# Two transformer blocks with expert layers: the end of the second mixer in a fixed order, rows stored as normed, scale and shift behind the gather

## The chip, the cores and the metric

The kernel runs on one core of a Trainium2 chip as one program. The metric is the device time of one execution in microseconds. The kernel before takes 2361.54 us, the median of three runs (2360.82 to 2361.91).

## What is computed

512 tokens of 1024 features pass through two blocks. Each block is a mixer and an expert layer. The change works in the end of the second mixer, in the lists of both expert layers, and in how the second expert layer gets its tokens:

```python
y = merge_branches(o_a, o_b, g_a, g_b, w_out_a, w_out_b, w_o)   # ends in a projection by w_o
x = x + gt1 * rmsnorm(y, g_post_mix)
h2 = rmsnorm(x, g_pre_ffn) * (1 + sc2) + sh2
logits = h2 @ w_router + b_router
top_logits, top_e = lax.top_k(logits, 4)                        # of 32 experts
top_w = softmax(top_logits)
f = sum over experts of top_w * (gated unit of (h2 @ w_gu + b_gu)) @ w_dn + b_dn, for its tokens
x = x + gt2 * rmsnorm(f, g_post_ffn)
```

The first expert layer has 16 experts, two for a token; the second has 32 experts of 12 weight pieces of 1 MB each.

## The kernel before

The stages run one after the other: first mixer, first experts, second mixer, second experts. Matmuls with full accuracy are made from three products: a weight piece is split into a high part (`whi`, a ScalarE copy, L120) and the rest (`wlo`, a VectorE subtraction, L121), the left side likewise, and TensorE multiplies high by high, high by low and low by high (`mm3`, L85).

**End of the second mixer** (`mixer2`, from L2152). The projection by w_o is made in eight blocks: two column halves, in each four blocks of 128 tokens (`out_mm`, L2171), 24 matmuls for a block. Behind a block ScalarE sums the squares and VectorE multiplies by a row of gains (`rows[0]`, L2178, L2179). `tail_norm` (L2182) waits for both halves of a block. VectorE adds the two sums and computes an inverse root (`rsqrt`, L146: a chain of small operations on VectorE, each waiting for the last), adds the residual (L2187); GpSimd multiplies by a second row (L2188) and stores the residual; ScalarE sums the squares again (L2192), and a second root follows (L2193). `tail_turn` (L2195) transposes a block by TensorE, copies it by ScalarE (L2199) and makes the 32 router logits (`logits`, L770). `tail_u` (L2203) applies root, scale and shift on VectorE and stores the finished rows to U2 through GpSimd's DMA queue. Then come top-8 for each block (`top8`, L787), the routing weights, one-hot masks and their sums (`weights_of`, L799), and `lists` (L812): positions of the tokens in each expert by matmuls with a triangle, and, in `aux`, each token's number and its weight in three bf16 parts (`w3`, L918). This part is not in a manual order: a scheduler orders it, mixed with the next stage.

**Expert stages** (`experts`, L1302). The expert order and all steps are written out by hand, as a list of weight pieces `seq` and of hooks at steps; step 0 is the first piece, and steps below 0 run ahead of the first matmul. Weight pieces go into eleven buffers of 1 MB in the second stage. Four of the first ten loads are issued at step -11 on GpSimd's queue, the others on SP's (`AHEAD`, `BEHIND`). The first expert (two in the first stage) has a fixed place. For it `prep` (step -17) makes the one-hot tile (`list_hot`, L926) from the positions, `prep2` (-14) sums with `aux` by TensorE (`list_sum`, L933), `prep3` (-13) makes the row indices and weights (`list_end`, L940), and `x_gather` (-12, L994) gathers the rows by an indirect DMA from GpSimd. `prep` also has GpSimd make the tile `bsel` (L2267) that selects the expert's bias lane. `x_turn` (L999) transposes four of eight column groups into PSUM at steps -4 and -2, and `x_split` (L1010) half a step later copies them to the high part by ScalarE and subtracts by VectorE; blocks of 64 or 32 tokens (`col`) are only copied by ScalarE. The `plan` (L842), a generator, orders the other experts by their counts, on GpSimd with TensorE transposes and matmuls; its pieces run at the steps of `PLAN`, and the loads of the other experts wait for the number `exi` that it writes. The 32 places of the second stage take 128 tokens (four of them, two with a second block of 64), 96 (ten), 64 (ten) or 32 (eight).

## Time and profile before

| | us |
|---|---|
| median of three runs | 2361.54 |
| the profiled execution | 2365.56 |
| its span, first to last instruction | 2363.7 |
| TensorE, VectorE, ScalarE, GpSimd busy in it | 2118.9, 1385.6, 1024.0, 432.8 |
| HBM read and written in it | 642 MB and 35 MB |

Times below are microseconds from the span's start. The page cuts the span into 40 slices of 59.1 us; a digit is a busy share in tenths. In a timeline, a row has its start, its length, the engine, the line, the operation and `out<-in`, with sizes in partitions by elements; a bracket gives the idle time before it and what ended that. Rows of a window give the busy time of each engine with the count of instructions, the granted share of TensorE's full clock, the mean busy share of the 16 DMA engines and GB/s. Copies between engines appear under the helper's line, so `L83` is any matmul and the tile names tell which.

### The profile page before, as it was taken

How to read it: one execution, taken by the hardware profiler on the slowest of the kernel's cores; microseconds unless marked ns; L12 is line 12 of the kernel's file. 1: busy time of each engine (PE TensorE's matmuls, PEld its weight loads, DVE VectorE, ACT ScalarE, POOL GpSimd, SP SyncE). 2: the span in 40 equal slices, each digit the busy share in tenths (PEclk: the TensorE clock that was granted, in tenths of full speed). 3: DMA queues.
4: the chain of work that ended last, by engine and by line, in shares of the span. 5: the costliest groups of instructions: out<-in, count | busy, mean ns of one | idle time of the engine just before them, and what ended most of it. 6: DMA issues, size and time to landing. Idle time of an engine off the chain costs nothing. (4 is left out here: it accounts for less than half of the span.)

```text
span 2363.7 us, 31489 instructions
## 1 busy us (share of the span) xinstructions
PE 2118.9 (90%) x11221; PEld 1357.3 (57%) x11221; DVE 1385.6 (59%) x2687; ACT 1024.0 (43%) x1560; POOL 432.8 (18%) x405
## 2 busy tenths in 40 slices
PE   6999996779997999999987989979999997999993
PEld 2656664446665887778865445635555563554551
DVE  5555597645786856664466456545455553654663
ACT  3332454435674544553234444424344433443553
POOL 2001223311312120000024211312211031112100
PEclk9999896989998999999997999989999998999996
DMA  9766446998986423313357999999999989999996
GB/s 291 241 205 237 177 172 257 353 355 309 356 292 205 103 76 111 109 58 118 130 181 282 383 405 399 363 375 403 403 395 395 405 342 379 403 401 398 398 409 229
DMA packets 174659, 679.80 MB, mean 288 GB/s; under 512 B 21293, under 2 KB 61061, under 8 KB 116129
## 3 DMA queue, kind: packets, MB, share of 16 engines
q1 hardware_dynamic: 151632, 606.83, 67.5%
q0 software_dynamic: 22576, 69.85, 10.6%
q8 instruction: 90, 1.47, 0.3%
q10 hardware_dynamic: 288, 1.05, 0.1%
q14 instruction: 73, 0.59, 0.1%
HBM read 642.29 MB, written 35.46 MB: 287 GB/s over the span
## 5 line engine op out<-in xcount | busy, mean ns | idle before, releaser
L121 DVE TENSOR_TENSOR wlo<-wraw,whi 128x1024 fp32r<-128x1024 f32 (+1 forms) x535 | 646.3, 1232 | 333.7 <-ACT whi L120 324.6
L120 ACT ACTIVATE whi<-wraw 128x1024 fp32r<-128x1024 f32 (+1 forms) x535 | 552.6, 1055 | 344.5 <-PE pm L83 124.7
L83 PE MATMUL pm<-whi,xh 128*96 128x512 f32 (+1 forms) x704 | 283.9, 404 | 15.1 <-ACT whi L120 15.0
L83 PE MATMUL pm<-wlo,xh 128*96 128x512 f32 (+1 forms) x704 | 281.0, 402 | 6.1 <-DVE wlo L121 5.5
L83 PE MATMUL pm<-wraw,xh 128*32 128x512 f32 (+1 forms) x1344 | 238.3, 617 | 12.6 <-DMA wraw<-in_w_gu 12.6
L83 PE MATMUL pm<-whi,xl 128*96 128x512 f32 (+1 forms) x608 | 243.0, 400 | 0.0
L996 POOL DMA_INDIRECT xg<-U,ig x52 | 88.5, 1701 | 631.2 <-issue 275.8
L1240 POOL DMA_INDIRECT Y<-eo,isc x52 | 99.2, 1908 | 402.8 <-ACT eo L1239 103.2
L83 PEld LDWEIGHTS pm<-whi,xh 128*96 128x96 f32 (+1 forms) x704 | 125.3, 178 | 64.3 <-ACT whi L120 20.4
L83 PEld LDWEIGHTS pm<-wraw,xh 128*32 128x32 f32 (+1 forms) x1344 | 68.1, 126 | 151.3 <-issue 124.0
L83 PEld LDWEIGHTS pm<-wlo,xh 128*96 128x96 f32 (+1 forms) x704 | 119.6, 170 | 50.3 <-DVE wlo L121 8.8
L83 PE MATMUL po<-wlo,ah 128*96 128x512 f32 (+1 forms) x304 | 124.2, 409 | 12.7 <-DVE wlo L121 12.4
L83 PE MATMUL po<-wraw,ah 128*32 128x512 f32 (+1 forms) x672 | 132.6, 620 | 1.9 <-DMA wraw<-in_w_dn 1.9
L83 PE MATMUL po<-whi,ah 128*96 128x512 f32 (+1 forms) x304 | 126.8, 417 | 8.1 <-ACT whi L120 6.3
L83 PEld LDWEIGHTS pm<-whi,xl 128*96 128x96 f32 (+1 forms) x608 | 106.4, 175 | 36.8
L83 PE MATMUL po<-whi,al 128*96 128x512 f32 (+1 forms) x304 | 121.8, 401 | 0.8 <-DVE al L1204 0.8
L1008 PEld LDWEIGHTS pt<-ident,xg 64*128 64x128 f32 (+3 forms) x416 | 56.5, 199 | 100.8 <-issue 51.8
L1008 PE MATMUL pt<-ident,xg 64*128 64x64 f32 (+3 forms) x416 | 70.0, 294 | 47.8 <-DMA xg<-U,ig 47.1
L1017 ACT ACTIVATE xh<-pt 128x384 fp32r<-128x384 f32 (+2 forms) x56 | 28.2, 504 | 130.1 <-PE pt L1008 114.8
L83 PE MATMUL px<-hh,whi 128*128 128x512 f32 x192 | 77.3, 403 | 0.6 <-DVE gsum L766 0.6
L83 PE MATMUL px<-hh,wlo 128*128 128x512 f32 x192 | 76.6, 399 | 0.0
L83 PE MATMUL px<-hl,whi 128*128 128x512 f32 x192 | 76.6, 399 | 0.0
(630 smaller groups left out, 3774.1 us busy)
## 6 DMA issues: line engine op xcount, KB each, us to landing
wraw<-in_w_gu SPq DMA_DIRECT2D x254, 1024.0 KB
wraw<-in_w_dn SPq DMA_DIRECT2D x126, 1024.0 KB
wraw<-in_w_e_down SPq DMA_DIRECT2D x31, 1024.0 KB
wraw<-in_w_e_gate SPq DMA_DIRECT2D x30, 1024.0 KB
wraw<-in_w_e_up SPq DMA_DIRECT2D x30, 1024.0 KB
wraw<-in_w_in SPq DMA_DIRECT2D x58, 512.0 KB
mz<-in_w_ada SPq DMA_DIRECT2D x80, 256.0 KB
wraw<-in_w_mod SPq DMA_DIRECT2D x26, 512.0 KB
```

The source lines that it names most:

```text
L83: self.nc.tensor.matmul(out, lhsT, rhs, start=start, stop=stop)
L120: nc.scalar.activation(h, v, AF.Copy)
L121: nc.vector.tensor_sub(l, v, h.bitcast(F32))
L996: self.nc.gpsimd.indirect_dma_start(out=B.xg[0:B.n, :], out_offset=None, in_=self.U, in_offset=bass.IndirectOffsetOnAxis(ap=B.ig[:, :1], a ...
L1008: self.nc.tensor.transpose(B.xt[:, k * n:k * n + n], B.xg[0:n, 4 * h2 + k:1024:8], self.ident[0:n, 0:n])
L1017: nc.scalar.activation(B.xh[:, d, 0:n], pv, AF.Copy)
L1240: nc.gpsimd.indirect_dma_start(out=self.Y[:, :], out_offset=bass.IndirectOffsetOnAxis(ap=B.isc[:, :1], axis=0), in_=o, in_offset=None, com ...
```

## The change

The end of the second mixer is written in one order for TensorE, VectorE, ScalarE and GpSimd (`manual_schedule` orders the instructions of the region for each engine; where those of other regions fall among them is left to the scheduler). The norms, transposes and logits of a block stand between the matmuls of later blocks. Two roots are made together (`root`), and one multiplication of the root is folded into its constants. The rows are stored as normed, by ScalarE, without scale and shift; the last two stores leave on SP's queue. Scale and shift are applied to the gathered and transposed rows in `x_split`, four VectorE operations for each half of a block, each with one column of scale and shift; the copy of `col` blocks by ScalarE goes. In both stages the indices of the fixed experts are made ahead of the routing weights (`lists_first`, `lists_comb`), and of the fixed experts' hooks only `prep` and `x_gather` are left. The plan's first four pieces move to steps -11 to -8, and until `exi` is written they run on VectorE in the second stage. The lane selectors are made at the start of the kernel. `warm` adds twelve small matmuls whose result nobody reads. The diff, cut:

```diff
@@ -31,7 +31,7 @@
-PLAN = {2: (-4, -3, -1, 0, 1, 2), 1: (-4, -3, -1, 0, 1, 2)}
+PLAN = {2: (-11, -10, -9, -8, 1, 2), 1: (-4, -3, -1, 0, 1, 2)}
 
...
+    def rsqrt_steps(self, v, n, eps, scale=1.0, out=None):
+
+
+        ve = self.nc.vector
         a, t, y0, y1, y2, y3 = [self.tiny.tile([128, 8], F32, name=f"rs{i}")[:, :n] for i in range(6)]
-        ve.tensor_scalar(a, v, scale, eps, op0=OP.mult, op1=OP.add)
-        ve.tensor_scalar(y0.bitcast(I32), a.bitcast(I32), -0.5, 1597463007.0, op0=OP.mult, op1=OP.add)
-        for i, (y, z, k) in enumerate(((y0, y1, 3.0), (y1, y2, 12.0), (y2, y3, 768.0))):
+        y3 = y3 if out is None else out
+        ve.tensor_scalar(a, v, -scale, -eps, op0=OP.mult, op1=OP.add)
+        yield
+        ve.tensor_scalar(y0.bitcast(I32), a.bitcast(I32), -0.5, 519682224.0, op0=OP.mult, op1=OP.add)
+        yield
+        for i, (y, z) in enumerate(((y0, y1), (y1, y2), (y2, y3))):
             if n == 1:
                 ve.scalar_tensor_tensor(t, y, a, y, op0=OP.mult, op1=OP.mult)
             else:
                 ve.tensor_mul(t, y, y)
+                yield
                 ve.tensor_mul(t, t, a)
-            if i == 2:
-                ve.tensor_scalar(y, y, -1.0 / 8192, None, op0=OP.mult)
-            ve.scalar_tensor_tensor(z, t, k, y, op0=OP.subtract, op1=OP.mult)
+            yield
+            ve.scalar_tensor_tensor(z, t, 3 * 0.5 ** (2 * (13 / 27, 4 / 9, 1 / 3)[i]), y, op0=OP.add, op1=OP.mult)
+            yield
         return y3
+
+    def rsqrt(self, *a, **kw):
+        return self.run_mod(self.rsqrt_steps(*a, **kw))
+
+    def together(self, *gs):
+
+        gs, r = list(gs), [None] * len(gs)
+        left = list(range(len(gs)))
+        while left:
+            for i in list(left):
+                try:
+                    next(gs[i])
+                except StopIteration as e:
+                    r[i] = e.value
+                    left.remove(i)
+        return r
...
+
+        self.ehalf = cp.tile([128, 2], F32, name="ehalf")
+        for s in range(2):
+            nc.vector.memset(self.ehalf[64 - 64 * s:128 - 64 * s, s:s + 1], -1.0)
+            for a in (2 * s, 2 * s + 1):
+                ps = slice(32 * a, 32 * a + 32)
+                nc.vector.tensor_scalar(self.ehalf[ps, s:s + 1], self.pcol[ps, :], -32.0 * a, None, op0=OP.add)
...
+    def warm(self, n):
+
+        ps = self.pt.tile([128, 512], F32, name="pt")
+        for _ in range(n):
+            self.mm(ps[:, 0:128], self.ident, self.ident, True, True)
+
...
+    def mask_steps(self, E, K, xf, oh, c0, n):
+
+        nc, cs = self.nc, slice(c0, c0 + n)
+        nc.vector.tensor_tensor(oh[:, cs], self.slots[:, None, None, 0:E].to_broadcast([128, n, K, E]),
+                                xf[:, cs, 0:K, None].to_broadcast([128, n, K, E]), op=OP.is_equal)
+        yield
+        with nc.allow_low_precision(reason="sums of zeros and a one"):
+            nc.vector.reduce_sum(self.L.mask[:, cs, :], oh[:, cs].rearrange("p c k e -> p c e k"), axis=AX)
+        yield
+
...
+    def lists_first(self, n, tile):
+
+        L = self.L
+        L.first, ohs, ps = [], [], []
+        for b in range(n):
+            ohs.append(self.list_hot(L.pos[:, :, b:b + 1], 128, tile(b)))
+            ps.append(self.list_sum(ohs[b], lambda c: L.aux[:, c, b, 0:3], 3))
+        for b in range(n):
+            L.first.append(self.list_rows(ps[b], 128, self.lsm, b))
+        return ohs
+
+    def lists_comb(self, ohs):
+
+        nc, L = self.nc, self.L
+        aux = L.aux
+        self.w3(aux[:, :, :, 3], aux[:, :, :, 4], aux[:, :, :, 5], L.comb, [128, 4, L.E])
+        for b, oh in enumerate(ohs):
+            ps = self.list_sum(oh, lambda c: aux[:, c, b, 3:6], 3)
+            w = self.lsm.tile([128, 1], F32, name=f"slw{b}")
+            nc.vector.reduce_sum(w, ps[:, 0:3], axis=AX)
+            L.first[b].append(w)
 
     def plan(self, fixed, pairs):
 
 
         nc, sm, L = self.nc, self.esm, self.L
-        ve, E = nc.gpsimd, L.E
+        ve, E = (nc.vector if L.E == 32 else nc.gpsimd), L.E
...
         if B.col:
-            nc.scalar.activation(B.xf[:, d, 0:n], pv, AF.Copy)
+            lo = B.xf[:, d, 0:n]
+        else:
+            lo = B.xh[:, d, n:2 * n] if B.dual else B.xl[:, d, 0:n]
+        if self.xcols:
+
+            g, s = self.xcols
+            f = lo if B.col else pv
+            for k in range(4):
+                j = 4 * h2 + k
+                nc.vector.tensor_scalar(f[:, k, :], pv[:, k, :], g[:, j:j + 1], s[:, j:j + 1], op0=OP.mult, op1=OP.add)
+            pv = f
+        elif B.col:
+            nc.scalar.activation(lo, pv, AF.Copy)
+        if B.col:
             return
         nc.scalar.activation(B.xh[:, d, 0:n], pv, AF.Copy)
-        lo = B.xh[:, d, n:2 * n] if B.dual else B.xl[:, d, 0:n]
...
+            if b < fixed:
+                B.ig, B.isc, B.w = L.first[b]
+            else:
+                B.oh = self.list_hot(pos, B.n)
...
                 for i, f in enumerate(((prep, b, B), (prep2, B), (prep3, B), (self.x_gather, B))):
-                    at(max(s0 - lead[i] - o, p0 + i), *f)
+                    if b >= fixed or i in (0, 3):
+                        at(max(s0 - lead[i] - o, p0 + i), *f)
...
-        mask, comb = self.weights_of(16, 2, ex, w, self.lsm, sm.tile([128, 128], F32, name="ohk"))
-        self.lists(16, mask, comb)
+        oh = sm.tile([128, 4, 2, 16], F32, name="ohk")
+        self.lists(16)
+        self.run_mod(self.mask_steps(16, 2, ex, oh, 0, 4))
+        self.lists_pos()
+        ohs = self.lists_first(FIXED[1], tile)
+        self.comb_of(16, 2, w, oh)
+        self.lists_comb(ohs)
 
...
-            nc.gpsimd.dma_start(self.dap(RW, n * 1024, [[8, 128], [1, 8]]), a)
+            if n != 1:
+                nc.gpsimd.dma_start(self.dap(RW, n * 1024, [[8, 128], [1, 8]]), a)
             ca.append(a)
-        R = self.router([(t["w_router_2"][0], t["b_router_2"], 0, 32)], sm, ca[1], self.col(self.mod2, 3, "rwc"))
+        self.xcols = ca[1], self.col(self.mod2, 3, "rwc")
+        R = self.router([(t["w_router_2"][0], t["b_router_2"], 0, 32)], sm, *self.xcols)
...
-        rows = [rt[:, i, :] for i in range(3)]
-        self.bcast_row(rows[0], self.dap(RW, 0, [[1, 1024]]))
-        self.bcast_row(rows[1], self.dap(RW, 1024, [[1, 1024]]))
-        self.bcast_row(rows[2], self.dap(self.mod2, 3 * 1024, [[1, 1024]]))
+        row = rt[:, 0, :]
+        self.bcast_row(row, self.dap(RW, 0, [[1, 1024]]))
...
-        rr = sm.tile([128, 4], F32, name="rr")
+            nc.vector.tensor_mul(d, ps, row[:, hf * 512:hf * 512 + 512])
+
+
+        nv = sm.tile([128, 5, 2], F32, name="nv")
+        nr = sm.tile([128, 5, 2], F32, name="nr")
+
+        def root(c):
+            a, b = (1 if c == 4 else 0), (1 if c == 0 else 2)
+            return self.rsqrt_steps(nv[:, c, a:b], b - a, 1e-6, 1.0 / 1024, nr[:, c, a:b])
+
+        def tail_sum(c):
+            nc.vector.tensor_add(nv[:, c, 0:1], ss[:, 2 * c:2 * c + 1], ss[:, 2 * c + 1:2 * c + 2])
+
         def tail_norm(c):
             cs = slice(c * 128, c * 128 + 128)
             yc = y[:, c, :]
-            nc.vector.tensor_add(ss[:, 2 * c:2 * c + 1], ss[:, 2 * c:2 * c + 1], ss[:, 2 * c + 1:2 * c + 2])
-            r = self.rsqrt(ss[:, 2 * c:2 * c + 1], 1, 1e-6, 1.0 / 1024)
-            nc.vector.scalar_tensor_tensor(yc, yc, r, xr[c // 2][:, c % 2, :], op0=OP.mult, op1=OP.add)
-            nc.gpsimd.tensor_mul(xr[c // 2][:, c % 2, :], yc, rows[1])
+            nc.vector.scalar_tensor_tensor(yc, yc, nr[:, c, 0:1], xr[c // 2][:, c % 2, :], op0=OP.mult, op1=OP.add)
 
             nc.gpsimd.dma_start(self.out[0, cs, :] if c % 2 else self.X3[c * 64:c * 64 + 128, :], yc)
             q = w4t("q4", 1024)
-            nc.scalar.activation(q, yc, AF.Square, accum_out=ss[:, 2 * c + 1:2 * c + 2])
-            nc.vector.tensor_copy(rr[:, c:c + 1], self.rsqrt(ss[:, 2 * c + 1:2 * c + 2], 1, 1e-6, 1.0 / 1024))
+            nc.scalar.activation(q, yc, AF.Square, accum_out=nv[:, c + 1, 1:2])
+
+        uTs = {}
 
         def tail_turn(c):
             uT = rt[:, 3, :] if c % 2 else bg.tile([128, 1024], F32, name="uT", tag="L")
-            uT = uT.rearrange("p (k q) -> p k q", k=8)
+            uT = uTs[c] = uT.rearrange("p (k q) -> p k q", k=8)
...
-            self.logits(R, c, uT, rr[:, c:c + 1])
+
+        def tail_logits(c):
+            w = pw.tile([128, 1024], F32, name="pw")
+            return self.logits_mm(R, uTs[c], w[:, 0:512], w[:, 512:1024])
+
+        def logit_end(c, ps):
+            nc.vector.scalar_tensor_tensor(R.lg[:, c, :], ps, nr[:, c + 1, 1:2], R.br, op0=OP.mult, op1=OP.add)
 
         def tail_u(c):
+
             q = xr[c // 2][:, c % 2, :]
-            nc.vector.scalar_tensor_tensor(q, q, rr[:, c:c + 1], rows[2], op0=OP.mult, op1=OP.add)
-            nc.gpsimd.dma_start(self.U2[c * 128:c * 128 + 128, :], q)
-
+            nc.scalar.activation(q, y[:, c, :], AF.Copy, scale=nr[:, c + 1, 1:2])
+            (nc.sync if c > 1 else nc.gpsimd).dma_start(self.U2[c * 128:c * 128 + 128, :], q)
+
+        L = self.lists(32)
+        top = self.top_tiles(sm, "r")
+        w = sm.tile([128, 4, 4], F32, name="rw4")
+        s = sm.tile([128, 4, 1], F32, name="rs4")
         W = wo_half(0)
         for c in range(4):
-            out_mm(c, 0, W)
+            out_end(c, 0, out_mm(c, 0, W))
         W = wo_half(1)
-        for c in range(5):
-            if c < 4:
-                out_mm(c, 1, W)
-            if c:
-                tail_norm(c - 1)
-        for c in range(4):
-            tail_turn(c)
-            tail_u(c)
-
-        lg = R.lg
-        em, ex = self.top8(lg, sm, "r")
-        w = sm.tile([128, 4, 4], F32, name="rw4")
-        s = sm.tile([128, 4, 1], F32, name="rs4")
-        nc.vector.tensor_tensor(w, em[:, :, 0:4], em[:, :, 0:1].to_broadcast([128, 4, 4]), op=OP.subtract)
-        nc.scalar.activation(w, w, AF.Exp)
-        nc.vector.reduce_sum(s[:, :, 0], w, axis=AX)
-        nc.vector.reciprocal(s, s)
-        nc.vector.tensor_tensor(w, w, s.to_broadcast([128, 4, 4]), op=OP.mult)
-        mask, comb = self.weights_of(32, 4, ex, w, self.lsm, w4t("ohk", 512))
-        self.lists(32, mask, comb)
+        with self.tc.manual_schedule(engines={ET.PE, ET.DVE, ET.Activation, ET.Pool}):
+            for c in range(2):
+                out_end(c, 1, out_mm(c, 1, W))
+            tail_sum(0)
+            self.run_mod(root(0))
+            tail_norm(0)
+            out_end(2, 1, out_mm(2, 1, W))
+            tail_sum(1)
+            self.run_mod(root(1))
+            tail_norm(1)
+            tail_turn(0)
+            ps = out_mm(3, 1, W, None, range(4))
+            l0 = tail_logits(0)
+            tail_turn(1)
+            tail_sum(2)
+            self.run_mod(root(2))
+            tail_norm(2)
+            logit_end(0, l0)
+            tail_u(0)
+            out_end(3, 1, out_mm(3, 1, W, ps, range(4, 8)))
+            l1 = tail_logits(1)
+            tail_turn(2)
+            tail_sum(3)
+            self.run_mod(root(3))
+            l2 = tail_logits(2)
+            tail_u(1)
+            tail_norm(3)
+            logit_end(1, l1)
+            logit_end(2, l2)
+            self.top8(R.lg, sm, "r", 0, 3, top)
+            tail_turn(3)
+            ohk = w4t("ohk", 4, 4, 32)
+            self.together(root(4), self.mask_steps(32, 4, top[2], ohk, 0, 3))
+            l3 = tail_logits(3)
+            self.warm(8)
+            logit_end(3, l3)
+            self.top8(R.lg, sm, "r", 3, 1, top)
+            self.run_mod(self.mask_steps(32, 4, top[2], ohk, 3, 1))
+            tail_u(2)
+            tail_u(3)
+            nc.vector.tensor_tensor(w, top[0][:, :, 0:4], top[0][:, :, 0:1].to_broadcast([128, 4, 4]), op=OP.subtract)
+            self.lists_pos()
+            self.warm(4)
+            nc.scalar.activation(w, w, AF.Exp)
+            ohs = self.lists_first(FIXED[2], lambda b: self.half_tile(w4t("loh", 1024)))
+            nc.vector.reduce_sum(s[:, :, 0], w, axis=AX)
+            nc.vector.reciprocal(s, s)
+            nc.vector.tensor_tensor(w, w, s.to_broadcast([128, 4, 4]), op=OP.mult)
+            self.comb_of(32, 4, w, ohk)
+            self.lists_comb(ohs)
```

`out_end` is the second half of the old `out_mm`, `logits_mm` the matmul part of `logits`, `lists_pos` the position part of `lists` with the counts copied by ScalarE, and `list_rows` is `list_end` without the weights.

## Rows read from the trace of the kernel before

**Rows 1.** The page's slices: mean busy share of the DMA engines.
```profile
DMA  9766446998986423313357999999999989999996
```

**Rows 2.** Windows: length, PE, PEld, DVE, ACT, POOL busy, clock, DMA share, GB/s.
```profile
1190.00:1222.00 32.00, 32.00 (x139) 25.86 (x138) 20.17 (x64) 9.65 (x18) 7.41 (x5) 1.00 0.37 128
1260.00:2337.00 1077.00, 993.56 (x4858) 557.51 (x4856) 589.17 (x819) 458.54 (x568) 212.46 (x156) 0.96 0.99 386
1520.00:1560.00 40.00, 39.25 (x223) 24.11 (x225) 20.32 (x31) 13.34 (x21) 9.25 (x8) 1.00 0.83 329
```

**Rows 3.** The same view, short stretches.
```profile
1245.00:1250.00 5.00, 0.25 (x4) 0.16 (x3) 4.74 (x16) 0.00 (x0) 3.31 (x4) 0.50 0.00 0
...
1265.00:1266.00 1.00, 1.00 (x6) 0.67 (x5) 0.23 (x1) 0.00 (x0) 0.00 (x0) 0.69 0.98 410
370.00:371.00 1.00, 0.00 (x0) 0.00 (x0) 0.93 (x8) 0.20 (x1) 0.00 (x0) 0.50 0.83 340
```

**Rows 4.** TensorE's timeline between the projection and the first expert matmul.
```profile
1222.05 0.40 PE L83 MATMUL px<-whi,ml 128*128 128x512 f32 x1
1222.29 1.05 PE L1618 MATMUL pt<-ident,y 128*128 128x128 f32 x8
...
1252.90 1.97 PE L1008 MATMUL pt<-ident,xg 128*128 128x128 f32 x8 [6.89 <-DMA xg<-U,ig]
...
1257.24 2.31 PE L83 MATMUL pt<-planm,plant 32*128 32x32 f32 x10 [0.72 <-ACT plant L869]
...
1260.07 0.63 PE L83 MATMUL pm<-whi,xh 128*128 128x512 f32 x1
```

**Rows 5.** VectorE's timeline at the end of the second mixer.
```profile
1206.51 0.69 DVE L2179 TENSOR_TENSOR y<-px,rows 128x512 f32<-128x512 f32 x1 [3.43 <-ACT q L2178]
...
1209.22 1.28 DVE L2187 SCALAR_TENSOR_TENSOR y<-y,rs,xr 128x1024 f32<-128x1024 f32 x1
...
1229.98 3.44 DVE L2205 SCALAR_TENSOR_TENSOR xr<-xr,rr,rows 128x1024 f32<-128x1024 f32 x1
...
1241.81 0.28 DVE L827 SCALAR_TENSOR_TENSOR pos<-px,mask 128x128 f32<-128x128 f32 x1
...
1246.56 0.15 DVE L950 CAST ig<-slf 128x1 int32<-128x1 f32 x1
```

**Rows 6.** GpSimd's timeline, first gather of the first stage and of the second.
```profile
376.55 1.05 POOL L996 DMA_INDIRECT xg<-U,ig  x1 [7.80 <-DVE slf L949]
...
1246.50 1.06 POOL L2267 TENSOR_SCALAR bsel<-ehalf 128x128 fp32r<-128x128 f32 x2 [8.60 <-DVE ehalf L2262]
1247.75 1.60 POOL L996 DMA_INDIRECT xg<-U,ig  x1 [0.18 <-issue]
1249.34 1.63 POOL L107 DMA_DIRECT2D wraw<-in_w_gu  x2
```

**Rows 7.** VectorE's timeline ahead of the first expert stage.
```profile
357.39 0.15 DVE L160 TENSOR_SCALAR rs<-rs 128x1 f32<-128x1 f32 x1
...
374.43 0.37 DVE L924 TENSOR_TENSOR aux<-w3r,aux 128x64 bf16<-128x64 f32 x1
...
375.54 0.15 DVE L950 CAST ig<-slf 128x1 int32<-128x1 f32 x1
```

**Rows 8.** ScalarE's timeline behind the projection.
```profile
1223.31 1.06 ACT L2192 ACTIVATE q<-y 128x1024 f32<-128x1024 f32 x1
...
1224.37 1.07 ACT L2199 ACTIVATE uT<-pt 128x512 f32<-128x512 f32 x2
```

**Rows 9.** SP's queue, last store of the first mixer.
```profile
368.77 0.32 SPq L698 DMA_DIRECT2D U<-u  x1
```

**Rows 10.** DMA issues from 1222 to 1250: count, size, us from issue to landing.
```profile
U<-xr POOLq DMA_DIRECT2D x3, 512.0 KB, 4.1
...
xg<-U,ig POOLq DMA_INDIRECT x1, 5.1
```

**Rows 11.** Groups by line in the second expert stage: count, busy us, mean ns.
```profile
L121 DVE TENSOR_TENSOR wlo<-wraw,whi 128x1024 fp32r<-128x1024 f32 x336 | 408.7, 1241 | 214.4 <-ACT whi L120 210.5
```

141 lines of the change are left out of this document (69 added, 72 removed).

## The prediction

> **What bounds the kernel now.** I read the slices first. From the 23rd slice on (1300 us), the DMA engines are busy nearly all the time [rows 1]; that is the second expert stage. Cut by stage, they are 99% busy from 1260 to 2337 us at 386 GB/s, while VectorE is busy for 589 of 1077 us [rows 2]. So this stage takes as long as its weights take to arrive, except where the two experts with a second block hold TensorE: around the first of them the DMA share falls to 0.83 [rows 2], and once more around the other. Its end can only move if its stream starts earlier or gains holes.
>
> The stretch before it is the opposite. Between 1245 and 1250 us nothing moves at all [rows 3]. The last projection matmul starts at 1222.05 and ends some 0.4 us later (1222.45), and the first expert matmul starts at 1260.07 [rows 4]: 37.6 us. What ends last there is one chain: VectorE's norms, the top-8 and the lists, up to the token index at 1246.56 [rows 5]; then the gather at 1247.75 and behind it on the same queue four weight loads from 1249.34 [rows 6]; then the transposes of the gathered rows at 1252.90, and ten plan matmuls from 1257.24 that stand ahead of the first expert matmul on TensorE [rows 4].
>
> **The change, step by step.** All sums are made against the profiled execution (2365.56 us; the median of the three runs, 2361.54, is 4.0 lower), and I carry the difference over to the median.
>
> *First stage's lists.* Before, both index sums wait for the weight path that ends at 374.80, and the first index is done at 375.69 [rows 7]. After, they need only the hot tiles, and the cast of the mask is gone: about 1.4 us earlier by VectorE's order. The gather started 0.86 us behind the index, at 376.55 [rows 6], and no row shows why; if something else released it, the gain is nothing. Between 0 and 1.4 I take 1.0, nearer the index. Each root has one operation less (0.15 at 357.39 [rows 7], with its gap 0.2), twice on the chain into the first router: 0.4. In the kernel's last root, 0.1.
>
> *The projection, in fixed order.* Its 139 matmuls in 32 us [rows 2] are 0.23 us each, so a block of 24 is 5.6 us, block 0 ends at 1205.65 and block 2 at 1216.8, as before. A block's multiply on VectorE ends 1.6 us behind its matmuls (block 0: 1207.2 [rows 5]), 1.7 where another square is ahead on ScalarE: 1218.5. From there to the residual add the sum and the root took 2.0 (1209.22 [rows 5]); for two columns it is a sum and eleven operations, some 2.3: 1220.8. The add is 1.28 [rows 5]: 1222.1. Now ScalarE's order counts: the square of block 1 (1.06) is written ahead of the transposed copies of block 0 (two in 1.07) [rows 8]. The first copy so ends at 1223.8, and TensorE, which has done eight transposes (1.05 [rows 4]) and half a block (2.8) by 1220.7, **waits 3.1 us** in front of router logits 0. With these logits (an estimated 1.8, half of it copy and waits between engines) and the next transposes (1.05) ahead of the last half block, the projection ends at 1229.5, **7.0 us later** than now.
>
> *From there to the index.* Multiply 1.5 (1231.0), sum and root 2.3, add 1.28 (1234.5), two logits and three top-8 with their cast 2.1 (1236.6), fourth root beside the masks of three blocks 2.6 (1239.2), last logits and top-8 0.9, last mask 0.6, position matmuls and positions 1.0 (a step on PSUM takes 0.28 [rows 5]), hot tile 0.7, sums and three small operations 1.0: **1243.4**. In the kernel before, VectorE carries four scale-and-shift passes more on this chain, one of them stretched to 3.44 while GpSimd multiplies [rows 5]; they leave, with GpSimd's multiplies. The bsel operations on GpSimd that held the gather from 1246.71 to 1247.75 [rows 5, 6] have their lane selectors from the start of the kernel; the small operations that make these there lie beside the first loads.
>
> *A new wait in front of the gather.* The gather reads stored rows, and the last two stores now leave on SP's queue, the last when ScalarE has scaled block 3: 1239.2 plus 1.06, so 1240.3. The four weight loads queue behind the gather on GpSimd, so a late store delays them too. From below, the like store on SP in the first mixer is issued at 368.77 [rows 9] and its bytes stop by 371.00 [rows 3]: 2.2 us. From above, stores on GpSimd's queue land 4.1 us after issue [rows 10]. I take about 3, nearer SP's row: 1243.3, level with the index. The upper end costs 1.0. [...] So gather and loads start at 1243.4, **4.3 us earlier**, and with them the stream.
>
> *From the gather to the first expert matmul.* Now 12.3 us. After: VectorE has, behind the index, the row operations and the whole weight path (estimated at 4.9), the plan's first part 1.0, two weight splits of 1.24 [rows 11], plan 0.6, a third split and a copy 1.4: 1253.8. The plan's last matmul so ends near 1254.0. The rows land at 1248.5 (5.1 after issue [rows 10]) and wait for that, since the plan stands ahead of the transposes on TensorE. Four transposes take 1.0 (eight took 1.97 [rows 4]), **four scale-and-shift operations 1.0** (bounds 0.6, at 0.15 each like a one-column operation [rows 7], and 1.1, at 0.28 each like the position step [rows 5], the nearest row), ScalarE's copy 0.6 and the handovers 0.2: first matmul at 1256.8, so 13.4 us, 1.1 longer. [...] Net 4.3 for loads and TensorE alike.
>
> *In every expert block.* Eight scale-and-shift operations on VectorE; for the 64 and 32 token blocks ScalarE's copy goes. 34 blocks by 8 by 0.2 to 0.28 is 54 to 76 us more on an engine that is free for 488 of 1077 us [rows 2]. They lie four steps ahead of their block, so I take nothing: the stream is the cover, and without it they would cost up to 2.2 us a block.
>
> **Sum**: 1.0 + 0.4 + 4.3 + 0.1 = 5.8 us off 2365.56, and so off the median: **2355.7**.
>
> **The rivals.** *B, the projection does not wait.* If the copies of block 0 get to run ahead of the square of block 1, the 3.1 us come off the whole chain: 2352.6. For it: TensorE has the transposes done at 1217.9. Against: ScalarE's order is written out.
>
> [...]
>
> *D, slower.* The scale-and-shift operations become the last wait in the wide blocks. There each expert has 24 splits of 1.24 us on VectorE [rows 11], 30 us, close to the 33 us that its twelve loads of 1 MB take at 386 GB/s. 14 blocks of 96 or 128 rows and two second blocks by 8 by 0.28 is 36 us, if all were exposed. Above a sixth (5.8 of 36) the gain is gone; at half the time is 2355.7 + 18, about 2374. Against: the eleven buffers hold 30 us of stream, and narrow blocks without splits stand between.
>
> That the change does not do what it says I hold unlikely: its order is explicit, only durations are open.
>
> **How the numbers follow.** About 0.2% (4.7 us) is what a measurement of this kernel tells from no change. Forecast 0.52, B 0.22, C 0.15, D 0.11. The forecast's own spread (2353 to 2358.5, from the bounds of lists, store, clock and root) lies to seven tenths below 2356.8, the line for faster. Faster: 0.37 + 0.22 = 0.59; same: 0.15 + 0.15 = 0.30; slower 0.11. The range runs from B with the bounds in its favour (2348.5) to the upper end of C (2361.5) and leaves out D and a little of B and C.
>
> **What would show it.** Right: the projection's end some 7 us later within its stage, with a wait in front of the first logits; the gather 4 us earlier; the plan's matmuls ahead of the gathered rows' transposes; the DMA share in the expert stage as now. Wrong: no such wait (B); a gather released late by the store, or transposes released by the plan long after the rows landed and no earlier expert matmul (C); DMA holes in wide blocks, with TensorE waiting on splits that stand behind scale-and-shift (D).

## The result: about one per cent slower, and the profile after

The changed kernel takes 2385.51 us (median of five runs, 2380.74 to 2386.43) where the kernel before took 2361.54 beside it. The ratio is 1.0091, with a 95% interval from 1.0072 to 1.0110, so 21.5 us slower where 5.8 faster was forecast. The profiled execution took 2384.26 us with a span of 2382.0, against 2365.56 and 2363.7: 18.3 us to find.

**Where the stream lost time.** The slices of the DMA engines after, to be laid beside [rows 1], have a dent at the 26th slice (8 where it was 9) and a deeper one at the 33rd (7 where it was 8):

```profile
DMA  9767547998976433314447999899999979999997
```

The windows of after that answer to [rows 2], and one more around the second expert that has a second block (length, PE, PEld, DVE, ACT, POOL busy, clock, DMA share, GB/s):

```profile
1190.00:1222.00 32.00, 32.00 (x139) 25.78 (x138) 11.38 (x20) 8.15 (x15) 0.38 (x1) 1.00 0.36 120
1260.00:2337.00 1077.00, 989.35 (x4807) 560.70 (x4808) 672.51 (x1095) 442.97 (x528) 206.73 (x151) 0.95 0.98 384
1520.00:1560.00 40.00, 39.24 (x195) 26.26 (x195) 24.30 (x34) 15.88 (x20) 9.24 (x8) 1.00 0.73 265
1910.00:1980.00 70.00, 69.22 (x329) 45.60 (x328) 41.64 (x57) 29.76 (x37) 20.36 (x16) 1.00 0.75 272
```

The last of these windows in the kernel before:

```profile
1910.00:1980.00 70.00, 65.68 (x372) 39.16 (x368) 35.06 (x47) 24.32 (x35) 18.47 (x16) 0.99 0.89 347
```

Around 1520 the share fell from 0.83 to 0.73, around 1910 to 1980 from 0.89 to 0.75. I added up the GB/s of windows of 10 us and read, from the end backwards, when the same bytes were left. Against the kernel before, the stream was 5.2 us late when 410 MB were left, and 3.1 when 360 were. At the first expert with a second block it lost 10 (13.3 late at 310 MB), at the second 15 (from 9.1 at 200 MB to 23.7 at 155). Between these places it regained some: 13.4 at 290 MB became 9.1 at 200. That was odd, and I come back to it. VectorE's busy time in the stage rose by 83 us.

What held the loads back is seen on SP's queue, where a weight load waits for its buffer to come free. From 1900 to 1985 us (us in total, times, longest), after and then before:

```profile
SPq L107 <- DVE wlo L121: 47.5, 11, 10.5
```

```profile
SPq L107 <- DVE wlo L121: 29.3, 6, 10.6
```

These are waits for a buffer whose low part VectorE had not yet split off. Over the whole stage (1260 to 2340) they are 286.2 us after and 171.0 before.

**Where the rest went.** The second mixer, which the change does not edit before its end, was already late. The first multiplication by hh, the first row below, started 0.9 us later than before; the first matmul of the next part 3.3 later. TensorE's timeline after, with two of its five waits on weight splits in this stretch (3.8 us together; before it has three, 1.3 us):

```profile
770.15 0.47 PE L83 MATMUL px<-whi,hh 128*128 128x256 f32 x1
...
773.73 0.51 PE L83 MATMUL px<-whi,hh 128*128 128x256 f32 x2 [0.44 <-ACT whi L120]
775.26 0.39 PE L83 MATMUL px<-wlo,hh 128*128 128x256 f32 x1 [1.02 <-DVE wlo L121]
...
799.41 0.40 PE L83 MATMUL px<-hh,whi 128*128 128x512 f32 x1
```

and before:

```profile
769.27 0.47 PE L83 MATMUL px<-whi,hh 128*128 128x256 f32 x1
...
796.13 0.39 PE L83 MATMUL px<-hh,whi 128*128 128x512 f32 x1
```

By the multiply of block 0 it was 5.4 us late (1206.51 in [rows 5], now 1211.94). The end itself, VectorE's rows after, beside [rows 5]:

```profile
1211.94 0.69 DVE L2285 TENSOR_TENSOR y<-px,rows 128x512 f32<-128x512 f32 x1 [3.13 <-ACT q L2284]
...
1238.15 0.69 DVE L2285 TENSOR_TENSOR y<-px,rows 128x512 f32<-128x512 f32 x1 [5.82 <-ACT q L2284]
...
1250.39 0.29 DVE L886 SCALAR_TENSOR_TENSOR pos<-px,maskb 128x128 f32<-128x128 f32 x1 [1.70 <-PE px L83]
...
1252.41 0.15 DVE L1025 CAST ig<-slf 128x1 int32<-128x1 f32 x1
...
1264.38 1.78 DVE L1105 TENSOR_SCALAR pt<-pt,rwa,rwc 128x128 f32<-128x128 f32 x4 [0.49 <-PE pt L1089]
```

and TensorE's, beside [rows 4]:

```profile
1229.30 1.08 PE L83 MATMUL pw<-uT,wr 128*32 128x128 f32 x16 [3.31 <-ACT uT L2313]
...
1231.21 1.95 PE L1720 MATMUL pt<-ident,y 128*128 128x128 f32 x8
...
1246.56 3.54 PE L83 MATMUL pt<-ident 128*128 128x128 f32 x16
...
1260.99 2.31 PE L83 MATMUL pt<-planm,plant 32*128 32x32 f32 x10 [2.34 <-DVE planm L933]
1263.22 1.97 PE L1089 MATMUL pt<-ident,xg 128*128 128x128 f32 x8
1266.90 0.79 PE L83 MATMUL pm<-whi,xh 128*128 128x512 f32 x1 [1.27 <-ACT xh L1111]
```

The forecast wait in front of the first logits is there, 3.31 us for 3.1. Behind it TensorE's next transposes took 1.95 where eight took 1.05 in [rows 4], with a granted clock of 0.50 from 1230 to 1232. The first eight warming matmuls (16 instructions) took 3.54, and the position step waited 1.70 for TensorE, whose position matmuls stand behind them. From block 0's multiply to the index 40.5 us passed; it was 40.1 before, and 36.9 were forecast.

**What the engines waited for in the expert stage** (from 1260 to 2340 for ScalarE, 1300 to 2330 for TensorE; us in total, times, longest). After:

```profile
ACT xh L1111 <- DVE pt L1105: 142.1, 32, 16.9
...
PE pt L1238 <- DVE xl L1112: 23.6, 10, 3.6
```

Before:

```profile
ACT xh L1017 <- PE pt L1008: 73.8, 12, 13.6
...
PE pt L1145 <- DVE xl L1019: 5.6, 5, 1.2
```

In the wide blocks (96 and 128 tokens) ScalarE's copy of the high part waited for TensorE's transposes; now it waits for VectorE, about twice as long. TensorE waits four times as long for the low part of the rows.

### The profile page after: what moved, and what is told of

It is laid out like the page before. It is cut to its first block, busy times and chain, and to the rows that moved or that the text cites. A ratio compares the mean times of both kernels' runs of the same rounds, so it can differ in the third digit from the quotient of the medians.

```text
span 2382.0 us, 31736 instructions
## 1 busy us (share of the span) xinstructions
PE 2129.8 (89%) x11257; PEld 1367.0 (57%) x11257; DVE 1460.5 (61%) x2902; ACT 1016.8 (43%) x1530; POOL 415.0 (17%) x387
## 3 DMA queue, kind: packets, MB, share of 16 engines
q10 hardware_dynamic: 288, 1.05, 0.1%
## 5 line engine op out<-in xcount | busy, mean ns | idle before, releaser
L83 PEld LDWEIGHTS pm<-wlo,xh 128*96 128x96 f32 (+1 forms) x704 | 118.7, 169 | 51.3 <-DVE wlo L121 11.1
L83 PE MATMUL po<-wlo,ah 128*96 128x512 f32 (+1 forms) x304 | 128.5, 423 | 11.6 <-DVE wlo L121 11.3
L1105 DVE TENSOR_SCALAR pt<-pt,rwa,rwc 128x96 f32<-128x96 f32 (+2 forms) x128 | 49.7, 388 | 54.8 <-PE pt L1089 51.2
```

The costliest lines, as they stand in the source:

```text
L83: self.nc.tensor.matmul(out, lhsT, rhs, start=start, stop=stop)
L1105: nc.vector.tensor_scalar(f[:, k, :], pv[:, k, :], g[:, j:j + 1], s[:, j:j + 1], op0=OP.mult, op1=OP.add)
```

## The experiments

The theory (H): scale and shift on VectorE stand between the transposes and ScalarE's copy, both engines run in the order written (in the block shown below ScalarE stands idle 2.98 us in front of such a copy and makes four weight copies, 3.89 us, behind it without a wait), and where weight splits stand behind them TensorE falls behind. A second cause (O): the new root changes the order that the scheduler gives the unedited second mixer. Rivals: L, the stage suffers only from its late start; V, VectorE's total time counts, wherever it is spent. Each ratio is against the kernel before on the same chip, in the same rounds, so it is not the quotient of the two medians beside it.

| run | kernel | median us | before beside it | ratio, 95% interval |
|---|---|---|---|---|
| | the change | 2385.51 | 2361.54 | 1.0091 (1.0072 to 1.0110) |
| e1 | change, no scale and shift in the stage | 2356.49 | 2362.25 | 0.9985 (0.9972 to 0.9997) |
| e2 | change, old root everywhere | 2377.24 | 2362.25 | 1.0067 (1.0052 to 1.0081) |
| e3 | change, scale and shift on ScalarE | 2363.56 | 2362.25 | 1.0005 (0.9995 to 1.0015) |
| e4 | change, copy half a step later | 2377.62 | 2362.25 | 1.0070 (1.0049 to 1.0090) |
| e5 | before, new root | 2369.64 | 2364.78 | 1.0037 (1.0024 to 1.0050) |
| e6 | before, scale and shift on VectorE | 2384.05 | 2364.78 | 1.0091 (1.0078 to 1.0104) |
| e7 | e3, old root outside the fixed order | 2362.29 | 2364.78 | 0.9990 (0.9979 to 1.0000) |
| e8 | e7, two mends of the end | 2359.69 | 2364.78 | 0.9976 (0.9966 to 0.9987) |
| e9 | before, buffers moved by 32 bytes | 2358.66 | 2362.59 | 0.9981 (0.9969 to 0.9994) |
| e10 | change, buffers moved by 32 bytes | 2390.68 | 2362.59 | 1.0118 (1.0099 to 1.0136) |
| e11 | end of e8, finished rows stored | 2358.94 | 2362.59 | 0.9981 (0.9970 to 0.9992) |
| e12 | before, buffers at multiples of 256 | 2353.80 | 2365.41 | 0.9951 (0.9938 to 0.9964) |
| e13 | e8, first stage's buffers too | 2357.80 | 2365.41 | 0.9977 (0.9966 to 0.9989) |
| e14 | e11, first stage's buffers too | 2354.54 | 2365.41 | 0.9959 (0.9944 to 0.9975) |
| e15 | change, scale and shift in narrow blocks only | 2356.95 | 2365.41 | 0.9968 (0.9956 to 0.9981) |

### Scale and shift: e1, e3, e4, e6, e15

**e1**, the changed kernel without them:

```diff
-        self.xcols = ca[1], self.col(self.mod2, 3, "rwc")
+        self.xcols = None
```

> The changed kernel without scale and shift in the second expert stage (this part of the computation is left out; the router keeps its own). Theory H: the four scale-and-shift operations on VectorE stand between the transposes and ScalarE's copy, both engines work in order, and so each waits for the other; the stage lost 11.6 us by it in the trace (gather of the first expert +5.6, gather at the first DMA hole +12.3, last store +18.7, less what the late start gave). Then about 2373 to 2375, with DMA shares near 0.83 again around both pair experts. Rival L: the stage only suffers from its late start (first matmul 6.8 us later), which shrinks the reserve at the pair experts; then no more than 1.8 us (the four operations ahead of the first expert) come back, 2384.

Measured 0.9985: 25 us come back by the ratios (0.0106 of 2361.5), where H had 11 and L 1.8. L falls. With the operations gone the change is 3.5 us faster than before. That this lies near the 5.8 of the sum is chance: as the runs below show, e1 still carries 6 to 9 us that the new root costs, 6 to 12 that the place of its buffers gains, and an end that gains about nothing.

One wide block shows the mechanism. ScalarE's timeline after, at the copies of a block of 96 tokens:

```profile
1403.61 1.04 ACT L120 ACTIVATE whi<-wraw 128x1024 fp32r<-128x1024 f32 x1
1407.63 0.49 ACT L1111 ACTIVATE xh<-pt 128x384 fp32r<-128x384 f32 x1 [2.98 <-DVE pt L1105]
1408.01 3.89 ACT L120 ACTIVATE whi<-wraw 128x1024 fp32r<-128x1024 f32 x4
1415.91 0.49 ACT L1111 ACTIVATE xh<-pt 128x384 fp32r<-128x384 f32 x1 [4.01 <-DVE pt L1105]
```

VectorE and TensorE after, in the same stretch:

```profile
1404.68 1.23 DVE L121 TENSOR_TENSOR wlo<-wraw,whi 128x1024 fp32r<-128x1024 f32 x1 [0.98 <-ACT whi L120]
1405.94 1.65 DVE L1105 TENSOR_SCALAR pt<-pt,rwa,rwc 128x96 f32<-128x96 f32 x4
...
1410.84 3.48 DVE L121 TENSOR_TENSOR wlo<-wraw,whi 128x1024 fp32r<-128x1024 f32 x3
1414.24 1.64 DVE L1105 TENSOR_SCALAR pt<-pt,rwa,rwc 128x96 f32<-128x96 f32 x4
...
1413.05 0.63 PE L83 MATMUL po<-wlo,ah 128*96 128x512 f32 x1
...
1417.05 0.74 PE L1238 MATMUL pt<-ident,eb 64*128 64x64 f32 x4 [2.44 <-DVE xl L1112]
```

The same block in e1, ScalarE and TensorE:

```profile
1403.64 0.47 ACT L1111 ACTIVATE xh<-pt 128x384 fp32r<-128x384 f32 x1
...
1407.80 0.47 ACT L1111 ACTIVATE xh<-pt 128x384 fp32r<-128x384 f32 x1
...
1411.24 0.69 PE L1238 MATMUL pt<-ident,eb 64*128 64x64 f32 x4 [1.20 <-DVE xl L1112]
```

The first copy stands behind the same weight copy in both (1403.61 and 1402.69, each 1.04). In e1 it starts at once. After, it waits 2.98 us: VectorE first makes a low part, then the four operations (1.65 together), and only then may ScalarE go on to the weight copies for which VectorE's next splits wait. The second copy waits 4.01. TensorE waits for low parts (0.98 us until 1408.76, 0.79 until 1410.38) and then works with a granted clock of 0.50: matmuls of 512 columns start 0.43 us apart there (after, 1410.92 to 1413.48), and 0.23 in e1, where the clock stayed at 1.00. A short window in each, after first, then e1:

```profile
1411.00:1413.00 2.00, 2.00 (x6) 1.30 (x5) 2.00 (x2) 0.90 (x1) 0.00 (x0) 0.50 1.01 426
```

```profile
1405.00:1407.00 2.00, 1.95 (x13) 1.53 (x13) 1.98 (x3) 2.00 (x4) 0.00 (x0) 1.00 1.04 438
```

From the first copy to the transposes of eb it is 9.4 us after and 7.6 in e1; from the weight copy at 1403.61 and 1402.69 it is 13.4 and 8.6.

**e6**, the same operations alone on the kernel before:

```diff
+        if self.xcols:
+            g, s = self.xcols
+            f = lo if B.col else pv
+            for k in range(4):
+                nc.vector.tensor_scalar(f[:, k, :], pv[:, k, :], g[:, j:j + 1], s[:, j:j + 1], ...)
+            pv = f
```

> The kernel before with only the four scale-and-shift operations on VectorE added ahead of ScalarE's copy (its rows are then scaled and shifted twice). Theory H: they cost by themselves what they cost in the changed kernel, 29 us (2385.5 less 2356.5): 2386 to 2392, with DMA holes of some 15 us more around the two pair experts. Rival L: they only cost that much because the stage starts late; here, with the start of before, less than 10: 2364 to 2372.

Measured 1.0091, 21.5 us. H had foretold more, 29 us. So they cost this by themselves, with the start of before, and the holes are the same: in the window that showed 0.75 after and 0.89 before, e6 has

```profile
1910.00:1980.00 70.00, 69.28 (x329) 45.73 (x328) 40.12 (x56) 27.96 (x35) 20.37 (x16) 1.00 0.77 287
```

and e1 has

```profile
1910.00:1980.00 70.00, 64.18 (x366) 38.73 (x362) 33.58 (x47) 22.86 (x34) 16.99 (x15) 0.98 0.89 349
```

**e3**, on ScalarE:

```diff
-                nc.vector.tensor_scalar(f[:, k, :], pv[:, k, :], g[:, j:j + 1], s[:, j:j + 1], op0=OP.mult, op1=OP.add)
+                nc.scalar.activation(f[:, k, :], pv[:, k, :], AF.Identity, scale=g[:, j:j + 1], bias=s[:, j:j + 1])
```

> Scale and shift made by ScalarE (four activations with a column of scale and of shift in place of four VectorE operations), everything else as in the changed kernel. Theory H: ScalarE no longer waits for VectorE, so most of the 11.6 us come back: 2374 to 2377, ScalarE busier by some 60 us. Rival V (it is VectorE's total, 75 us more, that counts): also about 2374 to 2377. Rival L: 2384 to 2386. Where ScalarE's own longer queue delays the weight copies as much: no change.

Measured 1.0005: 20 of the 25 us come back, more than the expectation had. The operations are no shorter there: grouped by shape, 96 tokens in e3 and after,

```profile
L1105 ACT ACTIVATE pt<-pt,rwc,rwa 128x96 f32<-128x96 f32 x80 | 32.1, 401 | 38.3 <-PE pt L1089 36.2
```

```profile
L1105 DVE TENSOR_SCALAR pt<-pt,rwa,rwc 128x96 f32<-128x96 f32 x80 | 30.7, 384 | 34.7 <-PE pt L1089 32.4
```

So it is not the time of the operations that counted but whom they held up. V foretold the same number here, so it took the next two to part them.

**e4**, copy and subtraction half a step behind the operations, which stay on VectorE:

```diff
-                    at(i + 0.5, self.x_split, B, h2)
+                    at(i + 0.5, self.x_affine, B, h2)
+                    at(i + 1, self.x_split, B, h2)
```

> Scale and shift stay on VectorE, but ScalarE's copy and VectorE's subtraction follow half a step later, behind another weight split. Theory H: the copy finds its input done, the mutual waits (two of 2.98 and 4.01 us on ScalarE in one block at 1404 to 1416) go, and 5 to 11 us come back: 2375 to 2380. Rival V (VectorE's total): unchanged, 2384 to 2387. Rival L: unchanged.

Measured 1.0070: 5 us by the ratios, at the lower end of H, and its interval overlaps that of the change, so that even these 5 are not clear. In its profiled execution, a long one of 2385.40 us, the copies still waited, 2.03 us each in the same block, and TensorE waited 3.36 for VectorE in front of the transposes of eb. So the half step mends the hand-over in part at most. How much of the 25 us is the hand-over, and how much is VectorE being late in the wide blocks by its own work, no run parts.

**e15**, only in the blocks of 64 and 32 tokens:

```diff
-        if self.xcols:
+        if self.xcols and B.col:
```

> The changed kernel with scale and shift on VectorE for the blocks of 64 and 32 tokens alone; the blocks of 128 and 96 tokens and the second blocks leave them out. Theory H: the cost sits where weight splits and the hand-over to ScalarE stand behind these operations, in the wide blocks; then nearly all of the 29 us come back: 2357 to 2363, a ratio of 0.998 to 1.001. Rival V: it goes by the time added on VectorE; 18 of the 34 blocks, with some 2 us each, still run them (the narrow ones take 0.24 instead of 0.45 us an operation), so a third of the cost stays: 1.002 to 1.005.

Measured 0.9968, no worse than with none at all (0.9985). V falls: the operations of the narrow blocks (64 and 32 tokens) take 37.3 of the 87.0 us that scale and shift take in the change (303 and 335 ns each, and 384 and 418 in the wide ones, not the half that the expectation had), so V would have kept some 10 of the 25 us. Where no weight splits stand behind them, the operations cost nothing that can be measured. The whole price is in the 14 blocks of 96 and 128 tokens and the two second blocks.

### The root: e2, e5, e7

**e2**, the old root in the changed kernel, and **e5**, the new one in the kernel before:

```diff
-        for i, (y, z, k) in enumerate(((y0, y1, 3.0), (y1, y2, 12.0), (y2, y3, 768.0))):
...
-            if i == 2:
-                ve.tensor_scalar(y, y, -1.0 / 8192, None, op0=OP.mult)
+        for i, (y, z) in enumerate(((y0, y1), (y1, y2), (y2, y3))):
```

> The changed kernel with the old inverse root (one operation more each) everywhere. Theory O: the shorter root alone changed the order that the scheduler gives the unedited part of the second mixer, where the trace of after falls behind from 768 to 1206 us by 5.4 us. With the old root that order is the one of before, block 0's multiply is at about 1206.5 again, and the time falls by 5 to 6 us, to 2379 to 2381. Rival: the 5.4 us come from later weights (DMA), whatever the order, or are taken back at the pair experts; then 2385 to 2386.

> The kernel before with the new, shorter inverse root and nothing else of the change. Theory O: TensorE's order in the second mixer becomes that of the changed kernel, its stretch from 768 us on falls behind by 3 us at 796 and by 5 at 1206, and the time is 2367 to 2370. Rival (the root is only shorter, as the prediction had it; the 8 us of the last run with the old root come from elsewhere): 2361 to 2362.

Measured 1.0067 and 1.0037: taken out of the change the new root gives back 5.7 us, put alone into the kernel before it costs 8.7 (5.7 to 11.8). The second is clear of no difference; the first is less sure, for the intervals of e2 and of the change overlap. In the compiled programs the order of TensorE's instructions in the second mixer is the same in before and e2, and the same in after and e5, and the two differ. The stretch between the two rows shown above takes 26.9 us before and 26.8 in e2, 29.3 after and 29.4 in e5; in e5 the same wait stands in it:

```profile
779.72 0.39 PE L83 MATMUL px<-wlo,hh 128*128 128x256 f32 x1 [1.00 <-DVE wlo L121]
```

So 2.5 of the 6 to 9 us are seen there. The rest I did not find at one place; ahead of this stretch the runs already lie between 766 and 775 us.

**e7** keeps the new root only in the fixed order and e3's ScalarE operations.

```diff
-    def rsqrt(self, *a, **kw):
-        return self.run_mod(self.rsqrt_steps(*a, **kw))
+    def rsqrt(self, v, n, eps, scale=1.0):
+        ...
```

> The changed kernel with scale and shift on ScalarE and the old root outside the fixed order (the fixed order keeps the new one). If the two causes add up: 2363.6 less 6 to 8, so 2355.5 to 2358, faster than both kernels. If the late second mixer was hidden behind the holes at the pair experts: 2362 to 2364.

Measured 0.9990, against 1.0005 for e3: 3.5 us, less than the 6 to 8 of adding up, and not the nothing of the other reading; the two intervals touch, so this is weak.

### The end: e8, e11

**e8**:

```diff
-            tail_norm(1)
             tail_turn(0)
+            tail_norm(1)
...
-            self.warm(8)
...
-            self.warm(4)
```

> As the last one, and in the fixed order without the twelve warming matmuls, and with the transposed copies of block 0 ahead of the square of block 1 on ScalarE. Theory: in the trace of after the eight matmuls took 3.54 us at half clock and the position step waited 1.70 us for them, and TensorE waited 3.31 us for the copies; without both the index comes 2 to 4 us earlier, and the time is 2352 to 2356. Rival: the matmuls keep the clock up for the transposes behind them, and without them the gain is given back: no difference from the last one.

Measured 0.9976 against 0.9990; the two intervals overlap, so the 3 us rest on the trace as well. Block 0's multiply, the position step and the gather in e8:

```profile
1212.72 0.69 DVE L2300 TENSOR_TENSOR y<-px,rows 128x512 f32<-128x512 f32 x1 [3.41 <-ACT q L2299]
...
1246.89 0.29 DVE L901 SCALAR_TENSOR_TENSOR pos<-px,maskb 128x128 f32<-128x128 f32 x1 [0.20 <-PE px L83]
...
1248.92 0.15 DVE L1040 CAST ig<-slf 128x1 int32<-128x1 f32 x1
```

```profile
1250.09 1.52 POOL L1092 DMA_INDIRECT xg<-U,ig  x1 [7.33 <-DVE rw L2397]
```

From block 0's multiply to the index: 36.2 us, where the change has 40.5 and e7 38.2. The gather comes 37.4 behind it, 41.4 in the change and 41.2 before.

The 2.0 us between e7 and e8 come from the new order, for they lie ahead of the last block's multiply, where no warming matmul stands: it comes 23.1 us behind block 0's in e8 and 25.1 in e7, and from there to the position step both take 11.1. In e7 the warming matmuls are still there; the first eight took 2.03 us at a granted clock of 1.00 and the position step waited 0.18 us, where it waited 0.20 in e8 without them. That they cost something is shown only by the profiled execution of the change, where the clock was 0.50 from 1246 to 1249; taking them out gained nothing that can be seen. And the wait in front of the first logits moved rather than went:

```profile
1229.67 0.41 PE L83 MATMUL pw<-ssum,l 128*128 128x32 f32 x2 [2.33 <-DVE rs L152]
```

Here TensorE waits for the copy `l` of these logits, which ScalarE makes only at 1229.36, behind the square of block 1 (1228.31, 1.06).

**e11** stores finished rows, so nothing is scaled behind the gather:

```diff
+            nc.gpsimd.tensor_mul(xr[c // 2][:, c % 2, :], yc, rt[:, 1, :])
...
-            nc.scalar.activation(q, y[:, c, :], AF.Copy, scale=nr[:, c + 1, 1:2])
+            nc.vector.scalar_tensor_tensor(q, q, nr[:, c + 1, 1:2], rt[:, 2, :], op0=OP.mult, op1=OP.add)
```

> The changed kernel's order at the end (old root elsewhere, no warming matmuls, the copies of block 0 first), but rows stored with scale and shift: GpSimd multiplies a block by the row of scales behind its residual add, VectorE's multiply-add with the second root and the row of shifts takes the place of ScalarE's copy, and nothing is scaled behind the gather. Theory H: the expert stage then has no scale and shift on any engine; at the end two multiply-adds of 1.28 stand between the last mask and the last stores, so the gather comes 1 to 3 us later than in the version with ScalarE (ratio 0.9976), and 4 to 7 us come back in the stage: a ratio of 0.995 to 0.997. Rival: GpSimd's multiplications stretch VectorE's chain at the end (one pass took 3.44 instead of 1.28 in the kernel before) and the gain is gone: 0.998 to 1.000.

Measured 0.9981, as e8, where 4 to 7 us more were expected. What the stage wins the end gives back: the gather comes 44.8 us behind block 0's multiply, 7.4 later than in e8, where 1 to 3 were expected.

### The place of the weight buffers: e9, e10, e12, e13, e14

The odd regain of the stream. The 90 MB between the last 290 and the last 200 took 225.0, 223.8 and 223.6 us in before, e5 and e6, but 220.7 to 222.0 in the change and e1 to e4, e7 and e8: one per cent, without a hole in either, whatever the engines did. One thing differed by family that no line of the diff is about: the change alters the sizes of small tiles, and with them the address at which the weight buffers begin. **e9** and **e10** move them by an unused tile:

```diff
+        self.pad = cp.tile([128, 8], F32, name="pad")
+        nc.vector.memset(self.pad, 0.0)
```

> The kernel before with one unused constant tile of 32 bytes a partition. In the kernel before the weight buffers of the expert stages begin at byte 36512, 44704 ... of a partition (32 modulo 64), in the changed kernel at 36352, 44544 ... (0 modulo 64), because the lists and the lane selectors changed size; the tile moves those of before by 32 bytes and nothing else. Theory A: this is why, between the pair experts, the stream of every kernel made from the changed one ran 1 per cent faster (the same bytes took 221.1 to 222.0 us against 223.6 to 225.0 of those made from before). Then the expert stage gains some 10 us: 2350 to 2354 by before's 2361.5, a ratio of 0.995 to 0.996. Rival: something else in the changed kernel makes the stream faster; then no change, 1.000.

> The changed kernel with the same tile of 32 bytes, which moves its weight buffers from 0 to 32 modulo 64. Theory A: the stream gets 1 per cent slower; since holes at the pair experts hide a part of it, 4 to 10 us more: 2390 to 2396, a ratio of 1.011 to 1.015. Rival: no change, 1.009.

Measured 0.9981 and 1.0118: 4.5 us faster, half of what was expected, and 6.4 slower than the change, though the intervals of e10 and the change overlap. The 90 MB took 222.8 us in e9 and 224.5 in e10. **e12** puts all buffers of both expert stages on multiples of 256 bytes, **e13** and **e14** do so for the first stage of e8 and e11:

```diff
+        self.pad = cp.tile([128, 24], F32, name="pad")
...
+        if nh == 1:
+            self.nc.vector.memset(self.pool("pad", 1).tile([128, 48], F32, name="padm"), 0.0)
...
+            self.nc.vector.memset(self.esm.tile([128, 48], F32, name="pade"), 0.0)
```

> The kernel before with three unused pads (96, 192 and 192 bytes a partition) so that the weight buffers of both expert stages begin at multiples of 256 bytes; in the changed kernel those of the second stage do (36352, 44544 ...), in the kernel before they lie at 160 and 224 modulo 256, in the run with 32 bytes at 192 and 0. That run's stream was half way between the two families (222.8 us for the bytes that took 225.0 and 220.7). Theory A256: multiples of 256 are what counts; the stream takes 220.5 to 222 us, and with the first expert stage the kernel gains 9 to 14 us: a ratio of 0.994 to 0.996. Theory A64: multiples of 64 are enough, and the rest is something else; then as with 32 bytes, 0.998.

> The version with scale and shift on ScalarE, the old root elsewhere and the two mends of the end (0.9976), and a pad of 192 bytes that also moves the first expert stage's weight buffers from 64 to 0 modulo 256. Theory A256: the first stage's stream of 330 us gains some 0.5 to 1 per cent, 2 to 3 us, half of it perhaps hidden: 0.996 to 0.997. Rival: no change, 0.9976.

> The version with finished rows stored (0.9981) and the same pad of 192 bytes. Theory A256: 0.996 to 0.997. Rival: no change, 0.998.

Measured 0.9951, 0.9977 and 0.9959. The kernel before, with nothing but its buffers moved, is 11.6 us faster, and its 90 MB take 221.7. That lies within the 220.7 to 222.0 of the changed family, so the place accounts for the difference between the families. Three things limit this. Each of these times is from one execution. In the kernel before, the pads and tiles also move the first stage's weight buffers, so not all of the 11.6 us need come from the second expert stage. And they shift the small tiles that lie behind them. e13 shows no gain over e8; e14 gains 5 us over e11, with intervals that overlap. The stretch without holes, from 2000 to 2280, has 401 GB/s in before, 403 in e9, 405 in e12, and 397 in e10. The kernels whose buffers begin at multiples of 256 and which have no scale and shift on VectorE in wide blocks (e1, e3, e7, e8, e11, e13 to e15) have 405 to 407, those that have it (the change, e2, e4) 400 to 403. The rows of this stretch in before and e12:

```profile
2000.00:2280.00 280.00, 265.15 (x1251) 150.86 (x1252) 176.21 (x230) 139.92 (x165) 50.98 (x34) 0.97 1.02 401
```

```profile
2000.00:2280.00 280.00, 266.01 (x1264) 151.19 (x1264) 176.07 (x228) 138.04 (x163) 49.91 (x34) 0.98 1.02 405
```

The best versions are thus e12 and e14, both faster than both kernels, and not to be told apart from one another.

## Why the prediction was wrong

**In every expert block**: this is the step that failed. "They lie four steps ahead of their block, so I take nothing: the stream is the cover" priced 54 to 76 us of added VectorE work at 0 (it measured 87.0); it cost 21 (e6) to 25 us (e1), all of it in the wide blocks and the two second blocks (e15). The step had counted the time on VectorE against a mean over the stage (589 of 1077 us). What bears on it is the stretch: at the experts with a second block TensorE, not the stream, sets the pace (busy 65.68 of 70 us around the second of them already before), and the loads wait for buffers whose low parts VectorE splits late (47.5 us for 29.3), so what is late there leaves holes in the stream that nothing fills. The argument against rival D, that eleven buffers hold 30 us, counts only where buffers are free; in that stretch the loads stood waiting for one. The lead of four steps covered the operation itself, not the engine behind it: the copy that waited for it had weight copies queued behind it. This path is read from one block, and e3 and e4 bear it out in part; how much of the 21 to 25 us goes by it, and how much by VectorE's own added time in the wide blocks, stays open. Each operation was also taken at up to 0.28; in PSUM it measured 0.38 at 96 and 0.42 at 128 columns.

**Rival D** was the case that came. Its place (wide blocks, e15) and its sign (holes, TensorE waiting) were right. Its path was only half right: not merely splits behind scale and shift, but first ScalarE's copy behind them. Two thirds of its 36 us were exposed (of the 49.7 us that these operations really took, about half), its price at that would have been 2380. Its chance was 0.11, and the range left it out, because of the argument on the buffers. Rival B did not come. Of C's signs one is there: the rows landed near 1257.8, 4.4 behind the gather, and the transposes stood behind the plan until 1263.22. But that is 5.4 us, where the sum itself had 5.5; no expert matmul came earlier because the index did not.

**Each root has one operation less**, 0.4 us: the operation is gone, but the step looked at the root's own chain and not at what a scheduler does with a shorter one. It cost 6 to 9 us elsewhere.

**The projection 7.0 later, the index at 1243.4**: the wait was there with 3.31 us, right. But behind it TensorE came back at a granted clock of 0.50: 1.95 for transposes of 1.05, and the half block behind them started its matmuls 0.43 us apart until 1235.94, 4.4 us for the 2.8 of the sum. In the profiled run the warming matmuls, which the sum left out, held the position step for 1.70. The index came 40.5 us behind block 0's multiply for 36.9, and the gather no earlier than before for 4.3 earlier. With the order turned in e8 it is 36.2, though TensorE still waits 2.33 us there, and the gather comes 3.9 us earlier than before. The sum's other terms on this chain measured within some 0.4 us each.

**The store wait**: there is no sign of one. The last two stores were issued at 1247.12, and from 1251 to 1253 nothing moved. The gather started at 1253.39, 0.83 us behind the end of the index cast (1252.56); in the first stage it had been 0.86 behind before, and the sum took this over for that stage and left it out here. **From the gather to the first matmul**: 13.5 us for 13.4, by luck in part: the four operations took 1.78 for 1.0, and the plan's last matmul ended 9.9 behind the gather for 10.6. **The clock**: no run shows the 1.1 us that the sum's net 4.3 lets come back here; measured was 0.9. The granted clock, 0.50 from the first expert matmul on, rose between 1270 and 1271 (0.90 in that microsecond), 3.1 to 4.1 us behind the first expert matmul, where it had been 4.9 to 5.9. From that matmul to the first of the next group it took 5.1 us, and 6.0 before. **First stage's lists**: in the profiled run the gathered rows' transposes came 1.2 us earlier (380.99, now 379.75), but at the end of that stage (709) 0.1 was left; other runs start between 378 and 384, so the runs cannot tell this term from nothing.

**What no step saw**: the buffers' place, 6 us (e10) to 12 us (e12) in the change's favour. Laid together: 21 to 25 for scale and shift, 6 to 9 for the root, about nothing for the end, less 6 to 12, is 15 to 28; measured were 21.5.

## What to carry to other kernels

A piece of work that moves into a pipelined stage is not free because its engine is half idle: look for the stretch where another engine sets the pace, and for what is queued, in order, behind the instruction that will now wait. Where a scheduler orders the rest, a shorter operation can lengthen a stage that nobody edited, so run each part of a change alone, on the kernel before. And compare the addresses of the large buffers of two kernels before explaining a difference of one per cent.

## What the runs showed of the hardware that was not expected

**The address of a buffer in SBUF changes the rate of the stream.** Rows of 8 KB a partition arrive fastest in buffers that begin at a multiple of 256 bytes (e12, 221.7 us for 90 MB), in the middle at 192 and 0 modulo 256 (e9, 222.8), slowest at 160 and 224 (223.6 to 225.0 in before, e5 and e6) and at 32 (e10, 224.5). These are single executions: that multiples of 256 are best is clear, the order of the others is not. Why the place counts, no run shows.

**Scale and shift of one column in place in PSUM** took 418 ns at 128 columns and 384 at 96 on VectorE, and 428 and 401 on ScalarE; from PSUM to SBUF at 32 columns it was 303 and 371. A quarter of the columns still took about three quarters of the time on VectorE, and ScalarE was no faster at any of these widths.
